# A third PSUM bank for the attention scores, taken from the projections, and a later place for one normalisation

## Chip, cores and metric

The kernel runs on one core of a Trainium2 chip. The metric is the device time of one launch in microseconds (us), the median of several runs. A core has five engines that run side by side, each with its own queue of instructions: TensorE (PE in the profile; its weight loads are listed apart as PEld), VectorE (DVE), ScalarE (ACT), GpSimd (POOL) and SyncE (SP), which issues most DMAs. TensorE writes its results to PSUM, which has eight banks; each bank here holds one tile of 128 partitions by 512 float32.

## What is computed

One hybrid decoder layer on 2048 tokens of width 1024. The normalised input is projected once; one part of the columns goes to a stick-breaking attention with 16 heads of 64, the other to a chunked state-space mixer (SSD). Each branch is gated and normalised, and one output projection adds both to the input. Cut to what matters here:

```python
hn = rmsnorm(x, norm_w)
q, k, v, z_sb, z_ssd, xBC, dt_raw = split(hn @ w_in)
q = rmsnorm(q per head, q_norm_w); k = rmsnorm(k per head, k_norm_w)
z = einsum(q, k) * 0.125                      # per head, strictly causal
log_keep = where(mask, log_sigmoid(-z), 0)
rest = reverse_cumsum(log_keep) - log_keep
w = where(mask, exp(log_sigmoid(z) + rest), 0)
o_sb = einsum(w, v)
y_sb = rmsnorm(o_sb * silu(z_sb), sb_norm_w)
y_ssd = rmsnorm((ssd(xBC, dt_raw) + D * xs) * silu(z_ssd), ssd_norm_w)
out = x + concat(y_sb, y_ssd) @ w_out
```

## The kernel before

Tokens are handled in two halves H of 1024 tokens. The order of the stages is: preparation of the first half's input; SSD of the first half (convolutions, chunks, then the gate projections of that branch, L778 to L782); attention for both halves (L449 to L713); SSD of the second half; output projection in two branches (`out_part`, L727), the attention's first.

**PSUM.** All tiles of PSUM come from four rings of banks, L30: `z` has two banks, `t` two, `av` one, `pj` three. A tile takes the next bank of its ring, and its first matmul waits until the last reader of the tile that had the bank before is done. In attention, `z` holds scores, `t` transposes, `av` the output of a head, `pj` projections. Outside, `z` and `pj` also serve the convolutions (pairs of tiles, by turns in `pj` and `z`, L294), `z` both products of an SSD chunk (`yd` and `yo`, L395 and L396), `pj` all tiles of the output's first branch and, by turns with `z`, those of the second (L757, L801, L805).

**Attention** runs over 32 segments (H, p, q): half H, pair p of heads (8 pairs), and q, the first or second 512 tokens of the half. A segment handles both heads e of the pair for its 512 queries, against all blocks c of 512 keys up to its own, so a segment has 8, 16, 24 or 32 steps, for Q = 2H+q from 0 to 3. A step i consists of

- `z_step` (L594): the scores in a `z` bank by two matmuls (L601, L602; on the diagonal a third, L604); two sigmoids by ScalarE, `be` to SBUF (L606) and one in place in the bank (L607); a scan by VectorE that reads the bank and writes the weights `w` (L610). The scan is the last reader of the `z` bank.
- `t_step` (L615), six steps later (LAG): four transposes of `w` into a `t` bank (L619), read by a rounding copy on ScalarE, `th` (L622), and by a subtraction on VectorE, `tl` (L624), the last reader of the bank.
- `av_step` (L632), two more steps later: two matmuls into `av` (L636, L637). At a head's end ScalarE and VectorE read it out (L642, L643), and POOL multiplies by the gate `gz` (L644).

**The fill.** Between steps, small pieces of work for the next two segments are issued by a generator, `fill_for` (L563), at a pace that the planner at L664 to L705 sets from costs and due times written by hand; at a segment's end the rest is drained (L706). For the segment after next it runs `stage_a` (L456): four projection tiles in `pj`, 24 matmuls each (L473 to L475); each tile is read by three operations of ScalarE (L478 to L480), and VectorE sums squares (L481). At its end come DMAs of shifted values `vd` and a subtraction on POOL (L498), then the reciprocal roots (`rsqrt`, L98, on VectorE: L103, L104, and three rounds of L106 to L108, on 128x16) and the scaling of q and k by them (L502, 128x1024, in place). For the next segment it runs `gate` (L505), 24 matmuls to one `pj` tile, whose readers are L511 and L512; `gz` has two buffers. `stage_b` (L515) transposes and weighs q and k (L524 to L531). In the second half's segments with q=0 and p under 6, `gates1` adds two `pj` tiles for the SSD gate.

In a segment whose next one has q=1, the fill begins with the gate; then come 12 steps of `stage_a`, `stage_b`, and the rest. In the others it begins with the 12 steps of `stage_a`. POOL subtracts the rounded from the full weights as they arrive (L133).

The framework sets the order of instructions on each engine when the program is built. Program order gives the priority; an instruction whose operands or bank are not free by the framework's reckoning lets later ones of the same engine go first. On the chip each engine then keeps that order.

Of the kernel before, what the change touches and what calls it, by code (L numbers as in the profile page):

```python
# [26 lines left out]

V_QW, V_KW, V_CW, V_CB, V_D, V_SBW, V_SSW, V_AL, V_DTB, V_NW, V_N = 0, 1, 2, 50, 62, 70, 78, 86, 102, 118, 126

PSB = {"z": 2, "t": 2, "av": 1, "pj": 3}  # L30
LAG = 6
NA = 12
WKB = 6
# [13 lines left out]
def hybrid_layer_kernel(ctx: ExitStack, tc: tile.TileContext, x, norm_w, wA, wP0, wP, wZ, wdt, vec, w_out, out):  # L47
# [50 lines left out]
    def rsqrt(pool, ss, n, inv, tag):  # L98

        xv = pool.tile([P, n], F32, name=tag + "x")  # L100
        y = pool.tile([P, n], F32, name=tag + "y")
        t = pool.tile([P, n], F32, name=tag + "t")
        ve.tensor_scalar(xv, ss, inv, EPS, ALU.mult, ALU.add)  # L103
        ve.tensor_scalar(y.bitcast(I32), xv.bitcast(I32), -0.5, 1597463007.0, ALU.mult, ALU.add)  # L104
        for _ in range(3):
            ve.scalar_tensor_tensor(t, xv, -0.5, y, ALU.mult, ALU.mult)  # L106
            ve.tensor_mul(t, t, y)
            ve.scalar_tensor_tensor(y, t, 1.5, y, ALU.add, ALU.mult)  # L108
        return y
# [340 lines left out]
    def attention(ap_, wp, hp, hx):  # L450

        segs = [(H, p, q) for H in range(2) for p in range(NP) for q in range(2)]
        made, wts, wzs, rows, vrs, gzs = {}, {}, {}, {}, {}, {}
        hx1, nw1 = [], []

        def stage_a(H, p, q):  # L456
# [7 lines left out]
            raw = ap_.tile([P, 4, 256], F32, name="raw", bufs=2)  # L464
            ss = ap_.tile([P, 4, 4], F32, name="ss", bufs=2)

            n = 400 if (H, p) == (1, 0) else 384
            for t in range(4):
                pj = ps("pj")
# [15 lines left out]
            vd = ap_.tile([P, 4, P], F32, name="vd", bufs=1)  # L485
# [11 lines left out]
                nc.sync.dma_start(vb_d[p:p + 1, :], vr[P - 1:P, 3, :])  # L497
            gp.tensor_sub(vd, vr, vd)  # L498
            vrs[H, p] = vr
            r = rsqrt(ap_, ss.rearrange("p t g -> p (t g)"), 16, 1.0 / 64, "qk")  # L500
            rv = raw.rearrange("p t (g d) -> p (t g) d", d=64)
            ve.tensor_tensor(rv, rv, r.unsqueeze(2).broadcast_to([P, 16, 64]), op=ALU.mult)  # L502
            rows[H, p, q] = (vd, raw)

        def gate(H, p, q):  # L505
            if q == 0:
                wzs[H, p] = load_z(wp, p, 512, "z", 2, True)
            pj = ps("pj")
            yield from projector(hx if H == 0 else hx1)[1](pj, wzs[H, p], slice(0, P), q)
            gz = ap_.tile([P, 512], F32, name="gz", bufs=2)  # L510
            sc.activation(gz, pj, AF.Sigmoid)  # L511
            ve.tensor_mul(gz, pj, gz)  # L512
            gzs[H, p, q] = gz

        def stage_b(H, p, q):  # L515

            vd, raw = rows.pop((H, p, q))

            AB = [ap_.tile([P, 2, 512], F32R, name="AB", bufs=4) for _ in range(2)]
            M = [ap_.tile([P, 512], F32R, name="M", bufs=4) for _ in range(2)]  # L520
# [42 lines left out]
        def fill_for(n):  # L563
            H, p, q = segs[n]
            if n + 1 == len(segs):
                return
            nx = segs[n + 1]
            if nx[2] == 1:
                yield from gate(*nx)
            rest = iter(())  # L570
            if n + 2 < len(segs):
                nn = segs[n + 2]
                if nn[:2] == (1, 0):
                    if nn[2] == 0:
                        nw1.extend(load_nw1(ap_))
                    xs = [scaled_x(ap_, nn[2] * 4 + i, nw1) for i in range(2)]
                    yield from stage_b(*nx)
                    yield from prep1(nn[2], hp, ap_, nw1, xs, hx1)
                rest = stage_a(*nn)
                for _ in range(NA if n else 0):  # L580
                    next(rest)
                    yield
            if nx not in made:
                yield from stage_b(*nx)
            if nx[2] == 0:
                yield from gate(*nx)
            if H == 1 and q == 0 and p < NJ:
                yield from gates1(p)
            yield from rest
# [195 lines left out]
    with tc.tile_pool(name="sp1", bufs=1, side="right") as sp:  # L785
        chunks, gates, _ = ssd(1, sp, wp, *projector(hx))
# [67 lines left out]
```

## Time and profile before

| | us |
|---|---|
| median of three runs | 2747.02 (2743.16 to 2747.48) |
| profiled execution, its own time | 2747.84 |
| its span, first to last instruction | 2745.6 |
| TensorE busy | 2592.6 (94%) |
| VectorE busy | 2016.6 (73%) |
| ScalarE busy | 1647.5 (60%) |
| GpSimd busy | 845.8 (31%) |

The granted TensorE clock is 0.988 of full speed as a mean over the span. Attention takes from about 345 to 2108 us, the first half of it up to about 1000. Times of instructions are counted from the span's start. A matmul's listed duration overlaps the next one's: two matmuls with 512 columns start 0.23 us apart, while each is listed with some 0.4 us. So a stage in which TensorE is shown as busy all the time can still have room, and the weight loads (PEld) with the idle time before them show better where it waits.

### The profile page before, as it was taken

The numbers are of one execution on the slowest core, as the hardware profiler recorded it, in microseconds if no ns is written. First come the engines' busy times: TensorE is split into PE (matmuls) and PEld (weight loads), VectorE is DVE, ScalarE is ACT, GpSimd is POOL, SyncE is SP. The second block draws the span as 40 slices with busy tenths as digits, with TensorE's granted clock in tenths as the row PEclk, the third lists the DMA queues.
The fourth block names the chain that finished last, engine by engine and source line by source line (L and its number), as shares of the span: only waits on it lengthen the run. The fifth ranks groups of instructions, "written<-read, shape, count | busy, mean of one in ns | idle before, by whom it ended". The sixth has DMA issues, their size and how long they took to land.

```text
span 2745.6 us, 40149 instructions
## 1 busy us (share of the span) xinstructions
PE 2592.6 (94%) x13858; PEld 2138.9 (78%) x13858; DVE 2016.6 (73%) x3160; ACT 1647.5 (60%) x3551; POOL 845.8 (31%) x844
## 2 busy tenths in 40 slices
PE   7998999999999999999999999999999896989999
PEld 5876788888888778787878787877776774778877
DVE  6566337767776777968696868688997667877766
ACT  4557446666666666868686867677886456331221
POOL 1456232322333222121212121212112456351553
PEclk9999999999999999999999999999999998999999
DMA  3225642222322422122212121222121136574553
GB/s 114 62 74 144 228 122 65 78 76 83 93 81 86 116 73 70 58 81 58 81 55 85 53 86 51 84 56 74 57 70 39 49 94 184 184 219 146 153 166 115
DMA packets 207627, 265.16 MB, mean 97 GB/s; under 512 B 18384, under 2 KB 127200, under 8 KB 207424
## 3 DMA queue, kind: packets, MB, share of 16 engines
q1 hardware_dynamic: 188992, 229.04, 28.1%
q10 hardware_dynamic: 18432, 33.56, 4.2%
q8 instruction: 109, 1.79, 0.3%
q14 instruction: 94, 0.77, 0.1%
HBM read 178.00 MB, written 59.38 MB: 86 GB/s over the span
## 4 chain that ended last, share of the span: by engine, by line
PE 53%; DVE 25%; issue 7%; ACT 7%; DMA 4%; POOL 3%; SPq 0%; ACTq 0%; DVEq 0%; POOLq 0%
DVE w L610 8%; PE t L619 5%; PE pj L475 4%; PE pj L474 4%; PE pj L473 4%; DVE tl L624 4%; PE pj L247 3%; PE pj L246 3%; PE pj L245 3%; PE av L636 3%; PE z L601 3%; PE av L637 2%; PE z L602 2%; PE pj L762 2%; PE pj L760 2%
## 5 line engine op out<-in xcount | busy, mean ns | idle before, releaser
L610 DVE TENSOR_TENSOR_SCAN w<-z,w,be 128x512 f32<-128x512 f32 x384 | 490.7, 1278 | 135.1 <-ACT z L607 132.5
L606 ACT ACTIVATE be<-z 128x512 f32<-128x512 f32 (+3 forms) x640 | 343.7, 537 | 328.9 <-PE z L604 166.0
L624 DVE TENSOR_TENSOR tl<-t,th 128x512 fp32r<-128x512 f32 (+3 forms) x640 | 376.9, 589 | 9.5 <-ACT th L622 7.6
L622 ACT CAST th<-t 128x512 fp32r<-128x512 f32 (+3 forms) x640 | 339.0, 530 | 31.8 <-PE t L619 29.5
L619 PE MATMUL t<-ident,w 128*128 128x128 f32 x2176 | 346.6, 275 | 9.8 <-DVE tl L624 3.8
L473 PE MATMUL pj<-wh,hh 128*128 128x384 f32 (+1 forms) x1024 | 349.9, 342 | 0.0
L475 PE MATMUL pj<-wh,hl 128*128 128x384 f32 (+1 forms) x1024 | 346.8, 339 | 0.0
L474 PE MATMUL pj<-wl,hh 128*128 128x384 f32 (+1 forms) x1024 | 346.7, 339 | 0.0
L607 ACT ACTIVATE z<-z 128x512 f32<-128x512 f32 (+3 forms) x640 | 341.1, 533 | 0.2
L610 DVE TENSOR_TENSOR_SCAN w<-z,be 128x128 f32<-128x128 f32 (+3 forms) x256 | 209.8, 819 | 170.3 <-ACT z L607 141.3
L619 PEld LDWEIGHTS t<-ident,w 128*128 128x128 f32 x2176 | 255.1, 141 | 71.7 <-DVE tl L624 16.7
L133 POOL TENSOR_TENSOR wl<-wraw,wh 128x384 fp32r<-128x384 f32 (+3 forms) x163 | 169.4, 1050 | 440.8 <-ACT wh L132 238.7
L644 POOL TENSOR_TENSOR y<-y,gz 64x512 f32<-64x512 f32 x64 | 82.9, 1296 | 531.1 <-DVE y L643 530.6
L473 PEld LDWEIGHTS pj<-wh,hh 128*128 128x128 f32 x1024 | 192.9, 188 | 12.5 <-ACT hh L173 0.2
L474 PEld LDWEIGHTS pj<-wl,hh 128*128 128x128 f32 x1024 | 193.0, 189 | 12.0
L475 PEld LDWEIGHTS pj<-wh,hl 128*128 128x128 f32 x1024 | 193.0, 188 | 0.7
L246 PE MATMUL pj<-hl,zh 128*128 128x512 f32 x432 | 175.3, 406 | 0.0
L245 PE MATMUL pj<-hh,zh 128*128 128x512 f32 x432 | 173.3, 401 | 0.0
L247 PE MATMUL pj<-hh,zl 128*128 128x512 f32 x432 | 172.2, 399 | 0.0
L636 PE MATMUL av<-th,V 128*128 128x512 f32 (+2 forms) x384 | 155.3, 405 | 12.1 <-DVE y L643 11.2
L601 PE MATMUL z<-M,AB 128*128 128x512 f32 (+2 forms) x384 | 141.4, 368 | 10.7 <-DVE w L610 8.5
L637 PE MATMUL av<-tl,V 128*128 128x512 f32 (+2 forms) x384 | 141.1, 368 | 0.0
(244 smaller groups left out, 6060.5 us busy)
## 6 DMA issues: line engine op xcount, KB each, us to landing
wraw<-in_wP_dram SPq DMA_DIRECT2D x112, 192.0 KB, 2.5
wk<-acs_scr SPq DMA_DIRECT2D x64, 256.0 KB, 3.4
AB<-AB SPq DMA_DIRECT2D x128, 128.0 KB, 2.4
Mc<-kc_scr ACTq DMA_DIRECT2D x64, 256.0 KB, 2.7
Vc<-vc_scr ACTq DMA_DIRECT2D x64, 256.0 KB, 2.6
wraw<-in_wZ_dram SPq DMA_DIRECT2D x54, 256.0 KB, 2.6
wraw<-in_wA_dram SPq DMA_DIRECT2D x44, 192.0 KB, 2.3
ea<-acs_scr SPq DMA_DIRECT2D x32, 256.0 KB, 4.4
```

What stands on the lines that cost most here:

```text
L245: te.matmul(pj[:m], a, hh[q][:, kt, :], start=(kt == 0), stop=False)
L246: te.matmul(pj[:m], a, hl[q][:, kt, :], start=False, stop=False)
L247: te.matmul(pj[:m], b, hh[q][:, kt, :], start=False, stop=(kt == KT - 1))
L473: te.matmul(pj[:, :n], a, wh[kt][:, 0:n], start=(kt == 0), stop=False)
L474: te.matmul(pj[:, :n], a, wl[kt][:, 0:n], start=False, stop=False)
L475: te.matmul(pj[:, :n], b, wh[kt][:, 0:n], start=False, stop=(kt == KT - 1))
L606: sc.activation(be[:, :nk], zp[:, :nk], AF.Sigmoid, scale=0.125)
L607: sc.activation(zp[:, :nk], zp[:, :nk], AF.Sigmoid, scale=-0.125)
L610: ve.tensor_tensor_scan(w[:, 0:nk][:, ::-1], zp[:, 0:nk][:, ::-1], be[:, 0:nk][:, ::-1], 0.0 if diag else prev[i][:, 0:1], ALU.mult, ALU.add)
L619: te.transpose(tp[:, i * P:(i + 1) * P], ws[i][:, j * P:(j + 1) * P], ident)
L622: sc.copy(th[:, rs], tp[:, rs])
L624: ve.tensor_tensor(tl[:, rs], tp[:, rs], f32(th[:, rs]), op=ALU.subtract)
```

## The change

The ring `z` gets three banks and `pj` two. The roots and the scaling at the end of `stage_a` become a function of their own, `norm_rows`. For q=0 it is called where it stood. For q=1 it is called at the beginning of the fill of the next segment (the one before the segment that the rows belong to), ahead of that segment's gate.

```diff
-PSB = {"z": 2, "t": 2, "av": 1, "pj": 3}
+PSB = {"z": 3, "t": 2, "av": 1, "pj": 2}
...
             gp.tensor_sub(vd, vr, vd)
             vrs[H, p] = vr
+            rows[H, p, q] = (vd, raw, ss)
+
+            if q == 0:
+                norm_rows(H, p, q)
+
+        def norm_rows(H, p, q):
+            vd, raw, ss = rows[H, p, q]
             r = rsqrt(ap_, ss.rearrange("p t g -> p (t g)"), 16, 1.0 / 64, "qk")
             rv = raw.rearrange("p t (g d) -> p (t g) d", d=64)
             ve.tensor_tensor(rv, rv, r.unsqueeze(2).broadcast_to([P, 16, 64]), op=ALU.mult)
-            rows[H, p, q] = (vd, raw)
...
-            vd, raw = rows.pop((H, p, q))
+            vd, raw, _ = rows.pop((H, p, q))
...
             nx = segs[n + 1]
             if nx[2] == 1:
+                norm_rows(*nx)
                 yield from gate(*nx)
```

## Rows read from the trace of the kernel before

**Rows 1.** The page's part 1: busy time, share, instructions of each engine.
```profile
PE 2592.6 (94%) x13858; PEld 2138.9 (78%) x13858; DVE 2016.6 (73%) x3160; ACT 1647.5 (60%) x3551; POOL 845.8 (31%) x844
```

**Rows 2.** Windows by stage: length, then busy us of PE, PEld, DVE, ACT, POOL.
```profile
345.00:920.00 575.00, 559.46 (x3263) 502.18 (x3262) 397.02 (x675) 357.12 (x863) 177.09 (x208) 1.00 0.30 85
1000.00:1890.00 890.00, 857.90 (x4769) 716.33 (x4767) 704.98 (x1012) 653.82 (x1406) 180.91 (x203) 1.00 0.24 69
1890.00:2108.00 218.00, 208.72 (x1124) 160.13 (x1123) 193.96 (x264) 171.57 (x358) 23.85 (x33) 1.00 0.19 53
```

**Rows 3.** PEld's waits: 1000 to 1880, 1880 to 2108, whole span (us, times, longest).
```profile
PEld z L601 <- DVE w L610: 59.8, 110, 1.9
...
PEld z L601 <- DVE w L610: 26.1, 55, 1.0
...
PEld t L619 <- DVE tl L624: 16.7, 46, 1.4
```

**Rows 4.** Windows in one head pair, a segment's end and the next head; columns as rows 2.
```profile
1428.00:1448.00 20.00, 18.49 (x95) 13.41 (x94) 19.90 (x35) 16.89 (x37) 9.29 (x11) 1.00 0.23 68
1448.00:1466.00 18.00, 18.00 (x104) 15.89 (x103) 10.91 (x15) 12.42 (x27) 4.68 (x5) 1.00 0.37 109
```

**Rows 5.** Timeline, DVE then PEld, at a segment's end: start, us, engine, instruction, [idle before].
```profile
1375.81 1.27 DVE L610 TENSOR_TENSOR_SCAN w<-z,w,be 128x512 f32<-128x512 f32 x1
1377.00 0.67 DVE L624 TENSOR_TENSOR tl<-t,th 128x512 fp32r<-128x512 f32 x1
1377.58 1.27 DVE L610 TENSOR_TENSOR_SCAN w<-z,w,be 128x512 f32<-128x512 f32 x1
...
1377.13 0.19 PEld L601 LDWEIGHTS z<-M,AB 128*128 128x128 f32 x1 [0.43 <-DVE w L610]
...
1377.71 0.48 PEld L619 LDWEIGHTS t<-ident,w 128*128 128x128 f32 x4
```

**Rows 6.** Timeline of DVE: the chain of roots for q=1, and the scan after it.
```profile
1431.64 0.17 DVE L103 TENSOR_SCALAR qkx<-ss 128x16 f32<-128x16 f32 x1
...
1440.72 1.20 DVE L502 TENSOR_TENSOR raw<-raw,qky 128x1024 f32<-128x1024 f32 x1
...
1442.44 1.27 DVE L610 TENSOR_TENSOR_SCAN w<-z,w,be 128x512 f32<-128x512 f32 x1
```

**Rows 7.** Timeline of DVE and POOL: L106 beside a weight subtraction and alone.
```profile
467.20 1.02 DVE L106 SCALAR_TENSOR_TENSOR qkt<-qkx,qky 128x16 f32<-128x16 f32 x1
...
469.42 0.17 DVE L106 SCALAR_TENSOR_TENSOR qkt<-qkx,qky 128x16 f32<-128x16 f32 x1
...
1449.08 1.02 POOL L133 TENSOR_TENSOR wl<-wraw,wh 128x384 fp32r<-128x384 f32 x1 [0.98 <-ACT wh L132]
```

**Rows 8.** PE's waits over the whole span: the SSD chunks' score bank.
```profile
PE z L412 <- DVE ea L419: 19.6, 10, 7.1
```

**Rows 9.** Timeline of PE and DVE in the output's first branch.
```profile
2438.49 0.47 PE L760 MATMUL pj<-hh,yh 128*128 128x512 f32 x1
...
2448.79 0.75 DVE L763 SCALAR_TENSOR_TENSOR res<-pj,roy,res 128x512 f32<-128x512 f32 x1
...
2449.59 0.80 PE L760 MATMUL pj<-hh,yh 128*128 128x512 f32 x1 [5.32 <-DVE res L763]
```

**Rows 10.** Timeline of PE and ACT in a first-half segment with q=0.
```profile
484.46 0.42 PE L473 MATMUL pj<-wh,hh 128*128 128x384 f32 x1
...
485.28 0.27 ACT L480 COPY vr<-pj 128x128 f32<-128x128 f32 x1
...
494.12 0.60 ACT L511 ACTIVATE gz<-pj 128x512 f32<-128x512 f32 x1 [1.87 <-POOL y L644]
```

**Rows 11.** Timeline of PE and DVE in a second-half segment with q=0.
```profile
1326.69 0.39 PE L245 MATMUL pj<-hh,zh 128*128 128x512 f32 x1
...
1330.36 0.69 DVE L512 TENSOR_TENSOR gz<-pj,gz 128x512 f32<-128x512 f32 x1 [0.62 <-ACT gz L511]
```

**Rows 12.** Timeline of ACT: a gate copy of the first half's SSD.
```profile
322.40 0.59 ACT L435 COPY zr<-pj 128x512 f32<-128x512 f32 x1 [8.30 <-DMA gss_scr<-zr]
```

## The prediction

> **What bounds the kernel now.** I read the page first: TensorE is busy 94% of the span, VectorE 73%, ScalarE 60%, GpSimd 31% [rows 1]. As matmuls overlap, the windows by stage say more [rows 2]. In attention's first half (345 to 920 us) TensorE loads weights 502 of 575 us and VectorE works 397: TensorE is the bound. In the second half (1000 to 1890) VectorE works 705 of 890 us, in the last two pairs (1890 to 2108) 194 of 218: there the bound changes inside each segment. Next, the waits: weight loads of the score matmuls (z) wait for the scan that frees a z bank, 59.8 us in 110 places between 1000 and 1880 and 26.1 us in 55 places after that, 86 us in all; over the whole span the transposes (t) wait only 16.7 us for `tl` [rows 3]. Windows inside one head pair (1328 to 1467 us) show the two regimes [rows 4]: at the end of a segment, when its fill has run out, VectorE works 19.90 of 20 us; at the head of the next, with dense fill, 10.91 of 18.
>
> **What a z wait is worth.** In the timeline of such an end [rows 5] one scan ends at 1377.08, z is loaded at 1377.13 after 0.43 us of idling; but the next transposes, at 1377.71, follow the end of a `tl` at 1377.67. That `tl` frees their t bank (two of them, L30). The step is 1.77 us (scan to scan), all VectorE's. With a third z bank z goes earlier, the transposes can't, and the period stays. I made this comparison for all 165 z waits after 1000 us; in 121 of them the transposes start within 0.15 us of the release of their bank. Where they start later, the smaller of wait and slack adds up to 11 us. So the third bank is worth between 0 and 11 us by this reading, 86 us if no other wait took over. I take 6.
>
> **The moved roots.** The chain L103 to L108 (11 small operations) and the scaling L502 is emitted for q=1 at the next segment's start instead of after its projections. It issues no DMA and moves past none; SP's and POOL's orders don't change by it; `vd` and its DMAs stay. What is behind it on VectorE are scans and `tl`. In [rows 6] it lies in the saturated end: from 1431.64 to the scan at 1442.44 are 10.80 us, in which five scans pass. At 1.77 us each, less 0.4 for one short `tl`, these need 8.5. So 2.3 us come free per such chain. It stands so in six segments (starts 1154 to 1848, one per pair; a seventh, 1977, moves within a stretch that is full everywhere, and those of the first half lie where VectorE has room). That is 6 x 2.3 = 14 us, at most 7 x 2.96 (its own time) = 21, at least 0 if the chain lands again among saturated scans. What it costs at the new place: the head leaves VectorE 18 - 10.9 = 7.1 us idle [rows 4]. But POOL subtracts weights there, from 1449.08 on, and beside such a subtraction an L106 took 1.02 us, alone 0.17 [rows 7]; chains in the first half, beside POOL, own 5.5 to 6.9 us. 5.5 still fit into 7.1. I cost it at nothing; what hides it is the wait of scans for the dense fill, and if that cover is gone it costs what it owns, 3 to 5.5 us a pair. The scaled q, k are wanted only 20 fill steps later.
>
> **Score banks outside attention.** The SSD chunks take yd and yo from z too; there z waits 19.6 us for `ea` [rows 8]. Three banks let the next group's yd start early, but these chunks also wait for ScalarE's exponentials and DMAs. Between 0 and 19.6 I take 5. The convolutions alternate z and pj in pairs, so one gains what the other loses: nothing.
>
> **The bank taken from the projections.** With three pj banks there is one TensorE wait, 5.3 us [rows 9]. The question is when three tiles were alive. I took each tile's first matmul and its last reader:
> - First half, segments with q=0: the gate tile's sigmoid waits for POOL's y and runs at 494.12, long after its matmuls [rows 10]. Until then four projection tiles share what is left: three banks leave two, two leave one. The tile at 484.46 starts while its predecessor is read until 485.55: 1.09 us. Such overlaps are 2.23, 1.09, 1.07 in each of six pairs, 26 us in all.
> - Second half: gates1's first tile starts at 1326.69, the gate tile before it is released at 1331.05, so 4.36 us [rows 11]; with 1.6 and 0.9 beside it 6.9 us, six times: 41 us.
> - These waits cost only if TensorE has nothing else. Instructions are ordered by readiness: at the end shown in [rows 4] the timeline has matmuls of the next segment's gate between score matmuls. Attention steps, 1.3 us of matmul work each, can go between two tiles. In the second half a fill pushed towards the saturated end costs nothing. Of 67 us I take 4.
> - First output branch: all tiles are pj. The tile at 2438.49 starts 11 us before the one at 2427 is released, 2449.54 [rows 9]; part of that is today's 5.3 us. The net loss here is 5.6 us, with a second such place (2468) near 10; the overlaps there sum to 28. I take 6.
> - First half's SSD gates: copies wait up to 8.30 us for the earlier store [rows 12]; overlaps sum to 14 us in five places. I take 4, since chunks fill some.
>
> **Sum**, against the profiled execution (2747.8 us, span 2745.6): -14 -6 -5 +4 +6 +4 = -11, so 2737. It stands 0.8 above the median, hence 2736.
>
> **Rivals.**
> 1. *Two banks serialise the projections* (slower). With the gate tile holding one bank, each projection waits for the predecessor's three ScalarE reads. For: [rows 10 to 12], and TensorE has no slack in the first half. Against: work that can go between. In full: 26 + 41 + 11 + 14 = 92 us; at half, with the gains of 25, +21: 2769. It decides from about a third of the 92 on. The Trainium skill, "Perfetto Trace Analysis", Matmuls, asks that independent matmul groups rotate through PSUM banks so that the evacuation of one overlaps the next group's matmuls; by that rule, taken strictly, the 92 us are lost: 92 - 25 = +67, 2814. No stretch of the trace shows pj at work with one bank, so it stays open. Chance 0.25.
> 2. *The chain isn't moved.* The ordering may pull these VectorE operations back among the saturated scans, as it does with the gate's matmuls. Then the 14 us don't come and the sum is +3: 2750. Chance 0.2.
> 3. *The z waits vanish.* If the transposes' 0.04 us in [rows 5] is only order and not a limit, most of the 86 us go: with half to three quarters of them the time is 2665 to 2710. The Trainium skill, "Perfetto Trace Analysis", Optimization Strategy, says that the same gap repeating on the engine that should be saturated can mean too few PSUM buffers; by that rule z's repeated gap would go with the third bank. Against it stands that in 121 of the 165 cases the t bank had just come free. Chance 0.1.
>
> **How the numbers follow.** My forecast, 2722 to 2743, has 0.45. A measurement tells some 0.2%, 5.5 us, from no change. Faster than 2741.5: nearly all of the forecast, rival 3, little of rival 2, 0.51. Within 0.2%: most of rival 2 and the rest of the forecast, 0.23. Slower: rival 1 and the tail of rival 2, 0.26. These have both signs, so the range reaches from the gains' far bounds (14 for the chain, 11 for the bank, 10 for chunks, no loss: -35, 2712) to rival 1 at somewhat under half (2766). The likeliest case's own range is 2722 to 2743.
>
> **What would show it.** Right: L502 of q=1 stands at the head of the next segment, beside idle scans; z waits on scans fall well under 86 us, and waits of t on `tl` rise by most of that; a pair of the second half is 2 to 3 us shorter than its 139. Wrong: TensorE waits at L473 or L245 for ScalarE's readers of pj, first-half pairs longer than now (rival 1); L106 to L108 of q=1 still between saturated scans (rival 2); t waits that stay near 17 us while pairs shrink by 5 or more (rival 3); output tiles that wait for L763 for over 15 us.

## The result, and the profile after

The change makes the kernel slower: 2775.32 us (median, 2773.84 to 2776.93) against 2747.25 for the kernel before, a ratio of 1.0107, 95% interval 1.0094 to 1.012. The forecast was 2736, its range 2712 to 2766: the sign was wrong, and the time lies 9 us above the range.

The new version's lines lie six or seven further down from L502 on: the scan is L617 (before L610), the subtraction for `tl` L631 (L624), the scores L608 (L601), the scaling of q and k L509 (L502), the output's sum L770 (L763). First the busy times, from the page's part 1, to be set beside [rows 1]:

```profile
PE 2617.0 (94%) x13858; PEld 2140.1 (77%) x13858; DVE 2025.3 (73%) x3160; ACT 1640.1 (59%) x3551; POOL 841.8 (30%) x844
```

The instructions are the same in number, and no engine has more than 1% more work, VectorE and the weight loads under 0.5%. What has grown, by 26.5 us (span 2772.1 against 2745.6), is time in which TensorE waits or goes on at a lower density (its listed busy time holds 24.4 us more for the same matmuls). The next table says where. It is worked out from the timelines of both kernels: the first stage ends where the first projection matmul L473 starts, a segment with the last addition to `y` (L643 before), and the means are over pairs 1 to 5 of the first half and 1 to 4 of the second, counted from 0, which differ among themselves by at most 0.4 us. In the stretches of these pairs the granted clock is 1.00 in both kernels. The addition that marks a segment's end comes some 21 us behind the first score matmul of the next segment, so work can move across the mark, and what counts in the second half is the sum of the two segments of a pair.

| us | before | after | difference |
|---|---|---|---|
| to the start of attention | 346.6 | 350.4 | +3.8 |
| attention | 1756.7 | 1780.1 | +23.4 |
| – of it, one pair of the first half | 76.70 | 78.23 | +1.53 |
| – of it, a first segment (q=0) of the second half | 63.53 | 65.04 | +1.51 |
| – of it, a second segment (q=1) there | 75.34 | 75.58 | +0.24 |
| from the end of attention | 642.3 | 641.6 | -0.7 |

**The projections wait.** In the first half, weight loads for L473 now wait for ScalarE's reading of an older projection tile, three times in a pair. These are the three places in the timeline of the weight loads (PEld) in one pair of the changed kernel; the bracket is the idle time before the load and what ended it. In between are lines without such a wait:

```profile
562.14 0.19 PEld L473 LDWEIGHTS pj<-wh,hh 128*128 128x128 f32 x1 [0.81 <-ACT vr L480]
...
568.46 0.19 PEld L473 LDWEIGHTS pj<-wh,hh 128*128 128x128 f32 x1 [0.41 <-ACT vr L480]
...
575.17 0.19 PEld L473 LDWEIGHTS pj<-wh,hh 128*128 128x128 f32 x1 [0.22 <-ACT vr L480]
```

They add up to 1.44 us, against the 1.53 by which the pair is longer. So there the loss is in plain sight.

**The scores' waits have become the transposes'.** PEld's waits in the changed kernel, first from 1020 to 1914 us, then to 2136 (about the same work as in the first two of [rows 3]; total us, times, longest), and at last three rows of the whole span:

```profile
PEld z L608 <- DVE w L617: 51.7, 78, 1.7
PEld t L626 <- DVE tl L631: 27.4, 58, 1.1
...
PEld z L608 <- DVE w L617: 17.2, 37, 1.0
PEld t L626 <- DVE tl L631: 9.7, 25, 0.9
...
PEld z L608 <- DVE w L617: 75.3, 121, 2.5
PEld t L626 <- DVE tl L631: 44.3, 98, 1.1
...
PEld pj L473 <- ACT vr L480: 12.1, 25, 1.1
```

Waits of z fell from 86 us to 51.7 + 17.2 = 69. Waits of t on `tl` grew over the whole span from 16.7 to 44.3. The 17 us gained at z are more than taken back at t.

**The chain of roots has stayed at the segment's end.** The timeline of VectorE in the changed kernel, with the first operation of a second segment's chain, one of the scans between, the last operation, and the scaling:

```profile
1452.71 0.18 DVE L103 TENSOR_SCALAR qkx<-ss 128x16 f32<-128x16 f32 x1
...
1457.66 1.27 DVE L617 TENSOR_TENSOR_SCAN w<-z,w,be 128x512 f32<-128x512 f32 x1
...
1469.05 0.15 DVE L108 SCALAR_TENSOR_TENSOR qky<-qkt,qky 128x16 f32<-128x16 f32 x1
1469.24 1.23 DVE L509 TENSOR_TENSOR raw<-raw,qky 128x1024 f32<-128x1024 f32 x1
```

Nine scans pass between L103 and L509, eight of the old segment and the first of the new one, where five passed in [rows 6]: the chain is spread more thinly, but still among the scans of the end. Windows of the changed kernel around such an end (the new segment's first score matmul starts at 1464.48) and for the head after it (length, then busy us of PE, PEld, DVE, ACT, POOL, as in [rows 4]) show the two regimes as before:

```profile
1451.00:1471.00 20.00, 18.27 (x95) 13.09 (x96) 19.86 (x34) 15.86 (x36) 7.07 (x9) 1.00 0.12 31
1471.00:1491.00 20.00, 19.56 (x109) 16.61 (x108) 13.60 (x18) 14.25 (x30) 7.68 (x9) 1.00 0.42 128
```

VectorE is full in the end (19.86 of 20 us) and has room in the head, which is where the chain was meant to run.

### The profile page after: what moved, and what is told of

Its sections match the earlier page's. It is cut to its first block, busy times and chain, and to the rows that moved or that the text cites. A ratio compares the mean times of both kernels' runs of the same rounds, so it can differ in the third digit from the quotient of the medians.

```text
span 2772.1 us, 40308 instructions
## 1 busy us (share of the span) xinstructions
PE 2617.0 (94%) x13858; PEld 2140.1 (77%) x13858; DVE 2025.3 (73%) x3160; ACT 1640.1 (59%) x3551; POOL 841.8 (30%) x844
## 4 chain that ended last, share of the span: by engine, by line
PE 55%; DVE 23%; ACT 7%; issue 6%; DMA 5%; POOL 3%; SPq 0%; ACTq 0%; DVEq 0%; POOLq 0%
DVE w L617 6%; PE t L626 5%; PE pj L473 5%; PE pj L475 5%; PE pj L474 5%; PE pj L245 4%; PE pj L246 4%; PE pj L247 4%; DVE tl L631 3%; PE av L643 3%; PE av L644 2%; PE z L608 2%; PE z L609 2%; PE pj L767 2%; PE pj L769 2%
## 5 line engine op out<-in xcount | busy, mean ns | idle before, releaser
L617 DVE TENSOR_TENSOR_SCAN w<-z,w,be 128x512 f32<-128x512 f32 x384 | 490.4, 1279 | 132.4 <-ACT z L614 129.4
L631 DVE TENSOR_TENSOR tl<-t,th 128x512 fp32r<-128x512 f32 (+3 forms) x640 | 376.8, 590 | 14.9 <-ACT th L629 12.5
L473 PE MATMUL pj<-wh,hh 128*128 128x384 f32 (+1 forms) x1024 | 352.8, 344 | 5.9 <-ACT vr L480 4.2
L475 PE MATMUL pj<-wh,hl 128*128 128x384 f32 (+1 forms) x1024 | 347.4, 339 | 0.0
L617 DVE TENSOR_TENSOR_SCAN w<-z,be 128x128 f32<-128x128 f32 (+3 forms) x256 | 209.0, 819 | 171.8 <-ACT z L614 144.9
L626 PEld LDWEIGHTS t<-ident,w 128*128 128x128 f32 x2176 | 251.4, 141 | 89.1 <-DVE tl L631 44.3
L133 POOL TENSOR_TENSOR wl<-wraw,wh 128x384 fp32r<-128x384 f32 (+3 forms) x163 | 169.5, 1052 | 458.1 <-ACT wh L132 254.0
L473 PEld LDWEIGHTS pj<-wh,hh 128*128 128x128 f32 x1024 | 193.1, 189 | 24.5 <-ACT vr L480 12.1
L475 PEld LDWEIGHTS pj<-wh,hl 128*128 128x128 f32 x1024 | 192.8, 188 | 1.5
L245 PE MATMUL pj<-hh,zh 128*128 128x512 f32 x432 | 174.4, 404 | 0.0
L247 PE MATMUL pj<-hh,zl 128*128 128x512 f32 x432 | 172.1, 398 | 0.0
L643 PE MATMUL av<-th,V 128*128 128x512 f32 (+2 forms) x384 | 156.3, 407 | 14.8 <-DVE y L650 14.1
L608 PE MATMUL z<-M,AB 128*128 128x512 f32 (+2 forms) x384 | 141.3, 368 | 6.6 <-DVE w L617 4.1
```

Source lines behind the costliest of these rows:

```text
L245: te.matmul(pj[:m], a, hh[q][:, kt, :], start=(kt == 0), stop=False)
L247: te.matmul(pj[:m], b, hh[q][:, kt, :], start=False, stop=(kt == KT - 1))
L473: te.matmul(pj[:, :n], a, wh[kt][:, 0:n], start=(kt == 0), stop=False)
L475: te.matmul(pj[:, :n], b, wh[kt][:, 0:n], start=False, stop=(kt == KT - 1))
L617: ve.tensor_tensor_scan(w[:, 0:nk][:, ::-1], zp[:, 0:nk][:, ::-1], be[:, 0:nk][:, ::-1], 0.0 if diag else prev[i][:, 0:1], ALU.mult, ALU.add)
L626: te.transpose(tp[:, i * P:(i + 1) * P], ws[i][:, j * P:(j + 1) * P], ident)
```

## The experiments

Twelve kernels, each timed against the kernel before. `attn` is the length of attention, first the time to its start and last the time behind it, all three from the traces by the same marks as above; the stage to the start of attention differs by 2 us (344.5 to 346.6) among six kernels in which nothing of it was changed, so differences of that size mean nothing there. Behind attention the spread among the same six is 4.8 us (637.5 to 642.3), and the three pairs of the first half that are not in the means add up to anything between 318.6 and 323.9. So a difference of up to 5 us in the whole of attention means little where the pairs don't show it too. The kernel before was timed again beside each group of runs, with medians of 2745.49 us (e1 to e4), 2744.07 (e5 to e8) and 2747.27 (e9 to e12); between groups, ratios compare, and not times.

| run | ratio [95%] | to attn | attn | behind | first-half pair | second half q=0 / q=1 |
|---|---|---|---|---|---|---|
| before | 1 | 346.6 | 1756.7 | 642.3 | 76.70 | 63.53 / 75.34 |
| after (the change) | 1.0107 [1.0094, 1.012] | 350.4 | 1780.1 | 641.6 | 78.23 | 65.04 / 75.58 |
| e1 banks only | 1.0079 [1.0066, 1.0092] | 349.9 | 1772.1 | 642.4 | 78.18 | 65.02 / 74.64 |
| e2 roots only | 1.0000 [0.9989, 1.001] | 344.9 | 1761.6 | 641.6 | 76.71 | 63.53 / 75.26 |
| e3 roots tied | 0.9977 [0.9967, 0.9988] | 344.9 | 1751.8 | 638.4 | 76.73 | 63.51 / 74.25 |
| e4 two pj banks only | 1.0111 [1.0094, 1.0128] | 350.9 | 1774.6 | 645.5 | 78.41 | 65.14 / 74.61 |
| e5 gate in z | 1.0066 [1.0054, 1.0078] | 350.3 | 1767.8 | 647.7 | 76.69 | 64.05 / 76.28 |
| e6 spread over z | 1.0163 [1.0146, 1.018] | 378.2 | 1764.4 | 644.0 | 76.70 | 63.82 / 76.08 |
| e7 roots tied, new banks | 1.007 [1.0057, 1.0083] | 347.4 | 1765.8 | 641.8 | 78.28 | 65.00 / 73.76 |
| e8 roots tied, old banks, 1.25 | 0.9952 [0.9941, 0.9964] | 346.4 | 1745.3 | 639.0 | 76.70 | 62.39 / 74.48 |
| e9 before with 1.25 | 1.0028 [1.0018, 1.0039] | 344.7 | 1769.4 | 639.1 | 76.73 | 62.39 / 77.82 |
| e10 roots tied, old banks, 1.15 | 0.9938 [0.9924, 0.9951] | 344.5 | 1741.5 | 637.5 | 76.67 | 63.54 / 72.93 |
| e11 gate's own bank | 1.0039 [1.0026, 1.0051] | 350.6 | 1757.7 | 647.2 | 76.73 | 63.86 / 75.33 |
| e12 third bank to t | 1.0061 [1.0048, 1.0073] | 352.6 | 1765.2 | 644.7 | 78.07 | 63.78 / 74.98 |

### The change in its parts: e1, e2 and e4

**e1** is the kernel before with the new banks alone:

```diff
-PSB = {"z": 2, "t": 2, "av": 1, "pj": 3}
+PSB = {"z": 3, "t": 2, "av": 1, "pj": 2}
```

> The kernel before with z 3 and pj 2 banks, the roots left where they were. Theory A (the bank costs, the moved roots do nothing because the ordering puts them back): as slow as the changed kernel, 2775 us, within 5. Rival B (the moved roots cost, by scans that wait behind them): near 2750 to 2760, the rest comes with the roots. In the first half's pairs theory A expects 1.4 us more a pair, all of it TensorE's wait for the last ScalarE reader of pj (L480).

**e2** has the moved roots alone, with the old banks (the rest of the diff ahead of the prediction).

> The kernel before with the roots of q=1 called in the next segment's fill, banks as before (z 2, pj 3). Theory A: no change, 2747 us, within 4, because the chain L103 to L108 still stands between the scans of the segment's saturated end. Rival B: 2765 or more. The prediction's term for the moved roots alone would give 2733.

**e4** takes the bank from the projections and gives it to nobody:

```diff
-PSB = {"z": 2, "t": 2, "av": 1, "pj": 3}
+PSB = {"z": 2, "t": 2, "av": 1, "pj": 2}
```

> The kernel before with pj 2 and z 2, one bank of PSUM unused. Theory A (the taken pj bank is the whole cost and the third z bank gives next to nothing, as the transposes' banks come free at the same time): 2775 us, within 5, and the same as with z 3. Rival C (the third z bank gives some 10 to 20 us and the pj bank costs 40 or more): 2785 to 2800. Rival D (z 3 itself costs, by another order of fill and scores): 2755 to 2765.

Measured: e1 2766.13 us, e2 2745.87, e4 2775.49. e1 and e4 divide attention's 23.4 us into steps: taking the bank from the projections costs 1774.6 - 1756.7 = 17.9 us (e4), giving it to the scores returns 1774.6 - 1772.1 = 2.5 (e1), and moving the roots on top of that costs 1780.1 - 1772.1 = 8.0 (the changed kernel against e1). Taken one after the other like this, steps always add up to the whole, so the sum tests nothing; e2 shows that moving the roots does less harm with the old banks. So the third bank for the scores is worth next to nothing in attention, 0.1 us in a pair of the second half and 0.2 in one of the first, and the projections' third bank is worth far more than that. Over the whole kernel the scores' bank brings more: the ratios of e4 and e1, 1.0111 and 1.0079, lie 9 us apart, and of the 6.6 us between their profiled executions 4.1 fall outside attention. Of the expectations, e2's theory A held, and e1 came out between its two; e4's theory A had the time right, but not that it would be the same as with the scores' third bank. PEld's waits of e1 from 1000 us to attention's end show the same exchange as the changed kernel's:

```profile
PEld z L601 <- DVE w L610: 64.0, 122, 1.3
PEld t L619 <- DVE tl L624: 32.0, 64, 1.4
```

and those of e4 in the same stretch:

```profile
PEld z L601 <- DVE w L610: 95.3, 178, 1.6
...
PEld t L619 <- DVE tl L624: 9.0, 35, 0.7
```

The sums, 96.0 and 104.3 us, differ by 8 us where the z waits alone differ by 31.

In e2 the chain lies where it does in the changed kernel, among the scans. Start and end of it in VectorE's timeline:

```profile
1434.08 0.17 DVE L103 TENSOR_SCALAR qkx<-ss 128x16 f32<-128x16 f32 x1
...
1449.55 0.14 DVE L108 SCALAR_TENSOR_TENSOR qky<-qkt,qky 128x16 f32<-128x16 f32 x1
1449.73 1.23 DVE L509 TENSOR_TENSOR raw<-raw,qky 128x1024 f32<-128x1024 f32 x1
```

From 1434.08 to 1450.87 lie nine scans. The later place in the program is a lower priority; that this is why the small operations end up thinly among the scans is a reading of the order, and not shown by a run. Pairs of the second half are 0.08 us shorter, which is nothing.

### The roots where the change's text puts them: e3 and e7

**e3** has the moved roots with the old banks, and ties the chain of a second segment behind the latest scan that has been issued, which is the first scan of the new segment (diff against e2).

```diff
-            r = rsqrt(ap_, ss.rearrange("p t g -> p (t g)"), 16, 1.0 / 64, "qk")
+            with tc.issue_after(scans[-1]) if q == 1 and scans else ExitStack():
+                r = rsqrt(ap_, ss.rearrange("p t g -> p (t g)"), 16, 1.0 / 64, "qk")
...
-            ve.tensor_tensor_scan(w[:, 0:nk][:, ::-1], zp[:, 0:nk][:, ::-1], be[:, 0:nk][:, ::-1],
+            sc_ = ve.tensor_tensor_scan(w[:, 0:nk][:, ::-1], zp[:, 0:nk][:, ::-1], be[:, 0:nk][:, ::-1],
...
+            scans.append(sc_.ins)
```

> As the one before, but VectorE's chain of roots is tied behind the first scan issued in the new segment, so that it can't be put among the earlier segment's last scans. If the term for the moved roots was right and only the ordering undid it, 6 chains x 2.3 us come free: 2733 us, and segments with q=1 of the second half are 2 us shorter than 75.3. If a full VectorE at a segment's end is not what sets its length, or the head pays it back: 2747, within 4.

Measured: 2740.2 us, 0.23% faster than before, with the interval below 1; that is between the two times expected. VectorE's timeline of e3 has the chain at the head, the scan of the new segment's diagonal block ahead of it:

```profile
1441.88 0.41 DVE L618 TENSOR_TENSOR_SCAN w<-z,be 128x128 f32<-128x128 f32 x1
1442.20 0.14 DVE L103 TENSOR_SCALAR qkx<-ss 128x16 f32<-128x16 f32 x1
...
1447.76 1.22 DVE L510 TENSOR_TENSOR raw<-raw,qky 128x1024 f32<-128x1024 f32 x1
```

So the move is worth something, but 4.9 us in attention and not 14. Why so little can be read from windows of the same length as the end of such a segment, from its last projection matmul (L473 to L475) to the next segment's first score matmul: 17.2 us in the kernel before (1428.3 to 1445.5), 15.3 in e3 (1424.4 to 1439.7). First the row of before, then, in a fence of its own, that of e3:

```profile
1428.30:1445.50 17.20, 15.97 (x81) 11.45 (x79) 17.10 (x32) 14.53 (x31) 7.11 (x9) 1.00 0.21 65
```

```profile
1424.40:1439.70 15.30, 14.41 (x76) 10.15 (x73) 14.94 (x20) 13.99 (x31) 6.01 (x8) 1.00 0.18 57
```

The end is 1.9 us shorter, near the 2.3 that the prediction works out. But in the kernel before TensorE does 12 matmuls of the next segment's gate (L245 to L247) in these 17.2 us, in e3 5. The seven that are left over are done in the head, where TensorE is the bound; at 0.23 us each, the distance of two matmuls with 512 columns, that would be 1.6 us. Of the 1.9 us the pair keeps 63.53 + 75.34 - 63.51 - 74.25 = 1.1. Where the other 0.8 us go shows when the stretch around the border is divided, for the kernels with and without the moved roots (us, medians of the second segments of pairs 1 to 4; the end is from the end of the last projection matmul to the next segment's first score matmul, the head from there to the segment's mark):

| run | end | gate matmuls in it | head |
|---|---|---|---|
| before | 16.42 | 12 | 21.48 |
| e2, roots moved | 15.27 | 5 | 22.40 |
| e3, moved and tied | 14.49 | 5 | 22.34 |
| e1, new banks | 14.65 | 10 | 22.29 |
| after, roots moved | 14.29 | 3 | 23.53 |
| e7, moved and tied | 12.62 | 3 | 23.38 |

In all four kernels with moved roots seven gate matmuls have left the end, and the head is 0.9 to 1.2 us longer than without. It is not the small operations of the chain that make it longer: all eleven lie in the head in e3 and e7, but only three in e2 and four in the changed kernel, each of 0.14 to 0.17 us (in the pairs whose chains are shown). What all four have there is the seven matmuls and the scaling, 1.2 us of VectorE. As VectorE has room in the head, the matmuls are the likelier cause, but no run separates the two.

**e7** has the same tie in the changed kernel, with its new banks.

> The changed kernel with its new banks, and the chain of the roots tied behind the first scan of the new segment, so that it stands where the change's code puts it. Theory (the 9 us between the run with the banks alone and the changed kernel come from the chain's ordering among the scans of the segment's end, and not from the idea of moving it): 2766 minus about 5, as the tie gave 5 without the banks, so about 2760, and a pair of the second half about 1 us shorter than in the changed kernel. Rival (the 9 us come from running the chain later at all, because fewer gate matmuls then fill the segment's end): the pair stays as in the changed kernel and the time within 3 us of 2775.

Measured: 2762.13 us, a ratio of 1.007, clear of the changed kernel's 1.0107; from e1's 1.0079 the intervals don't tell it apart. The second segments are 1.8 us shorter than in the changed kernel and 0.9 shorter than in e1. The last table says how. Against e1 the head grows by about the same in both, 1.2 us in the changed kernel and 1.1 in e7, while the end gets 2.0 us shorter in e7 and only 0.4 in the changed kernel. So the move costs the head something wherever the chain lands, and with the new banks it pays only if the chain leaves the end. The net loss in the changed kernel's attention thus belongs to the place that the ordering chose for the chain, and not to the idea of running it later; the rival of the expectation falls.

### Who needs the third projection bank: e5, e6 and e11

**e5** is e1 with the gate's tile of second segments in the scores' ring.

```diff
-            pj = ps("pj")
+            pj = ps("z" if q else "pj")
```

> Banks changed (three for the scores, two for the projections), roots where they were before, and the gate's projection of a pair's second segment takes a bank of the scores' ring in place of a projection bank. Theory (the projections lose their time because the gate's tile holds one of the two projection banks for the whole of its filling, so that the projections of the next pair have a single bank left): a pair of the first half goes back from 78.2 us towards the 76.7 of the kernel before, a first segment of a pair of the second half from 65.0 towards 63.5, and the time is some 10 to 15 us under the 2766 of the run with the banks alone, about 2753. Rival (two banks are too few for the q, k, v projections themselves, whoever else uses them): a pair of the first half stays at 78.2 and the time at 2766, or above it where the gate's tile now takes a bank from the scores.

Measured: 2762.08 us. The pair of the first half is back at 76.69, as the theory has it, to 0.01 us. First segments of the second half gain 1.0 of the 1.5. But second segments lose 1.6 against e1, so that the pair is 0.7 longer, and the whole gains some 4 us, not 10 to 15; the intervals of e5 and e1 overlap. PEld's waits of e5, from 1000 us to attention's end, show the gate's tile itself waiting for scans:

```profile
PEld z L601 <- DVE w L610: 65.8, 115, 1.5
PEld t L619 <- DVE tl L624: 37.3, 82, 1.5
...
PEld z L245 <- DVE w L610: 4.3, 9, 0.5
```

In the second half a bank lent by the scores is not free: the 4.3 us at L245 and 5.3 more at t than in e1 are the rival's part.

**e11** separates the two. One of the three projection banks is taken out of the ring and kept for the gates of second segments; all else is the kernel before.

```diff
-PSB = {"z": 2, "t": 2, "av": 1, "pj": 3}
+PSB = {"z": 2, "t": 2, "av": 1, "pj": 2, "gb": 1}
...
-            pj = ps("pj")
+            pj = ps("gb" if q else "pj")
```

> The kernel before with one of its three projection banks taken out of the ring and kept for the gates of second segments alone; two banks for the scores, roots where they were. Theory (the loss of the projections with two banks is the gate's tile, which holds one of them for its whole filling): 76.7 us for a pair of the first half and 63.5 and 75.3 for the two segments of a pair of the second half, as in the kernel before; only the first stage and the last keep their loss, so about 2752 to 2755. Rival (q, k and v need the third bank themselves): 78.2 and 65.0 as with two banks, 2770.

Measured: 2757.25 us, with 76.73, 63.86 and 75.33 in attention, which is 1.0 us longer in all than in the kernel before, where e4 is 17.9 longer. So in the first half q, k and v do with two banks; what they can't do with is one bank, and one is what the gate's tile leaves them while it is filled between other work and waits for its readers. That is [rows 10] read to its end: the gate's reader L511 came at 494.12, long after its matmuls. The remaining loss, 10 us, is outside attention, where the ring is two banks again and the gates' own bank lies unused: 4.0 in the first stage, and 4.9 behind attention, which is about the spread there. In e11's first stage one gate matmul waits 5.7 us for ScalarE's copy, [rows 12]'s line L435:

```profile
PEld pj L245 <- ACT zr L435: 5.7, 1, 5.7
```

**e6** is the changed kernel with all other users of `pj` lent a bank from `z`: the gates of second segments and of `gates1` as a whole, the first stage's gates and the first output branch by turns.

```diff
-            pj = ps("pj")
+            pj = ps(("pj", "z")[q] if m == P else "pj")
...
-        out_part(op0, op0, 0, ("pj",), wo)
+        out_part(op0, op0, 0, ("pj", "z"), wo)
```

> The changed kernel whole, and the users of the projection ring other than q, k and v spread over both rings: the gates of second segments and of the last stage's chunks go to the scores' ring, the gates of the first stage and the sums of the first output half take the two rings in turn. Theory (all of the loss of the smaller ring is waits for a bank, 25 us over the stages by the run with one bank unused): the first stage ends at about 345 to 347 us in place of 350, a pair of the first half takes 76.7 in place of 78.2, the last stage comes back by 3, and the time is 2750 to 2757, of which 5 to 9 over the kernel before are left for the moved roots. Rival (the scores' waits grow by as much when their ring is lent): 2770 or more.

Measured: 2787.86 us, the slowest of all. Attention is 15.7 us shorter than in the changed kernel, near what the theory wanted, but the first stage is 27.8 longer. There the SSD chunks take both their products from `z`, and a gate tile now stands between them. PEld's waits in the first stage of e6, 60 to 380 us:

```profile
PEld z L416 <- DVE ea L419: 28.2, 11, 6.6
```

In e1, with the same rings and the gates in `pj`, it is (60 to 352 us):

```profile
PEld z L416 <- DVE ea L419: 9.1, 10, 2.9
```

The waits are 19 us longer, against 27.8 us of the stage. For the rest there is one sign. From 260 to 300 us the granted clock was 0.81 in e6, so some two fifths of that stretch were at the lower of the two levels, 1.2 GHz, after 40 us in which TensorE was busy for 28.43; in the changed kernel it was 1.00, after 40 us with 35.86. What that took is not shown. A ring shared with slow readers hands their delay on to the others, whichever ring it is. The expectation was a miss on this stage.

### Where the bank could have gone: e12

```diff
-PSB = {"z": 2, "t": 2, "av": 1, "pj": 3}
+PSB = {"z": 2, "t": 3, "av": 1, "pj": 2}
```

> Two banks for the scores, two for the projections, and the bank that is left given to the ring of the transposes (three in place of two); roots where they were. Theory (the waits for a bank in the second half are VectorE's, which frees the scores' banks by its scans and the transposes' banks by its copies, so a bank more only changes which of the two TensorE waits for): second-half pairs within 0.5 us of the run with the eighth bank unused (65.1 and 74.6 us), waits of the transposes shorter and those of the scores longer, the whole 2765 to 2775. Rival (with three scores' banks the transposes' ring was what then held TensorE, so it is the one that wanted the bank): pairs at least 2 us shorter, 2755 or less.

Measured: 2763.28 us. Attention is 9.4 us shorter than with the bank unused (e4), where the scores' bank brought 2.5; a pair of the second half has 138.76 against 139.75, where e1 has 139.66. Over the whole kernel the intervals of e12 and e1 overlap, as e12 is slower outside attention. Neither side of the expectation holds: pairs are neither within 0.5 us nor 2 us shorter. And the prediction that z would wait longer was wrong. PEld's waits of e12 from 1000 us to attention's end, to be set beside e4's rows above:

```profile
PEld z L601 <- DVE w L610: 76.6, 153, 1.4
...
PEld t L619 <- DVE tl L624: 5.5, 9, 1.0
```

Both are shorter, 95.3 to 76.6 and 9.0 to 5.5. So VectorE isn't all that holds the second half, and of the two rings it is the transposes' that gains by a bank in attention. Which of its users does, whether the steps' or those of L524 (`stage_b`), was not tried. First segments of the second half are back at 63.78, as they are in e11 (63.86), though here the gate's tile shares two projection banks as in e4 (65.14). So in the second half a bank for the transposes makes up for that loss as well as one for the gate does; whether it takes the same loss away or brings a gain of its own is not shown. A pair of the first half stays at 78.07.

### The room in the ends: e8, e9 and e10

If a head that TensorE bounds is what the dense fill lengthens, then spreading the fill further into the end should pay once the chain has left the end, and only then. The planner's factor for the second half (`FF`) sets how fast the fill is spent. A lower factor spends it more slowly, so more of it is left for the end: the last projection matmul of a second segment ends 37.4 us behind the mark at which the segment starts in e3, 41.9 in e8 and 44.7 in e10. The expectation of e8 has this direction the wrong way round; its times don't hang on it. **e8** is e3 with a lower factor, **e9** the kernel before with the same one, **e10** e3 with one lower still.

```diff
-FF = (1.05, 1.35)
+FF = (1.05, 1.25)
```

> The run with the tied chain and the old banks (2740), with the factor of the planner for the second half lowered from 1.35 to 1.25, which spends the next segment's matmuls earlier and leaves fewer for the head. Theory (what a segment's end gives back is the number of gate matmuls that TensorE can do there: the kernel is TensorE-bound in heads, VectorE-bound in ends): more work planned into the ends, second-half pairs shorter by up to 1 us each, 2733 to 2738. Rival (the planner's factor already balances the two ends, so that earlier matmuls only delay scores): 2740 or slower, up to 2750.

> The kernel before with nothing but the planner's factor for the second half lowered from 1.35 to 1.25. Theory A (what the tied chain gives and what the factor gives are separate, each by where the fill is done): the factor alone gives the 8 us that lay between the run with the tied chain and the run with both, so about 2737. Theory B (the factor pays only where the chain has left the segment's end, since in the kernel before that end is full on VectorE): 2744 or slower, and second-half pairs of 138.5 us or more.

> The tied chain and the old banks once more, with the planner's factor for the second half at 1.15 in place of 1.25 and 1.35. If what limits the pair is TensorE in the head, with room left in the segment's end: another 4 to 8 us less, 2724 to 2728. If the room in the ends is used up at 1.25: 2732 or slower, with first segments of a pair shorter and second segments longer by as much or more.

Measured: e8 2731.95 us, e9 2754.03, e10 2729.92. The same edit takes 6.5 us off attention with the tied chain (e8 against e3) and adds 12.7 without it (by the ratios of the whole kernel, 7 and 8), so theory B of e9 holds: pairs there have 62.39 + 77.82 = 140.2 us. In e8 first segments are 1.1 us shorter than in e3 and second segments only 0.2 longer. What the slower fill costs a second segment differs, because in e9 the chain is still in the end. Windows of 20 us at the end of the same segment (columns as above) show how much TensorE does there. In e9 TensorE is busy 16.50 us, and the second segments are 2.5 us longer than before:

```profile
1430.00:1450.00 20.00, 16.50 (x86) 12.41 (x85) 18.71 (x31) 16.08 (x34) 9.66 (x11) 1.00 0.28 79
```

In e10 it is busy 19.66 us, with 111 matmuls in place of 86 and as much work of VectorE beside it:

```profile
1416.00:1436.00 20.00, 19.66 (x111) 16.38 (x111) 18.71 (x24) 18.80 (x43) 9.28 (x11) 1.00 0.27 80
```

e10's time lies between the two that were expected, and the intervals (0.9924 to 0.9951 and 0.9941 to 0.9964) don't tell it from e8. Its segments moved against the second expectation, first segments 1.1 us longer than in e8 and second segments 1.5 shorter. Either beats both kernels; e10 is 0.6% below the kernel before, and 1.7% below the changed one. It has the change's second part, tied in place, and a slower fill, without the first part.

## Why the prediction was wrong

By the ratios over the whole kernel, the bank taken from the projections cost 30 us (e4) where the prediction has 4 + 4 + 6 = 14; the bank given to the scores returned 9 (e1 against e4) where it has 11; the moved roots brought nothing with the old banks (e2) and cost 8 with the new ones (the changed kernel against e1) where it has a gain of 14.

**The bank taken from the projections** is the step that failed most: "Attention steps, 1.3 us of matmul work each, can go between two tiles. [...] Of 67 us I take 4." Attention lost 17.9 (e4). The place was named; but the discount to 4 rested on no row. In the first half 1.7 us of 4.4 overlapping in a pair were lost, since TensorE is the bound there and its order is set when the program is built: a load at L473 that waits for L480 holds all that stands behind it. In the second half first segments lost 1.6 and second segments won 0.7 back, so a pair lost 0.9. Only 3.0 us of the changed kernel's waits at L473 fall into the second half, so most of the loss there isn't seen as a wait for a bank. A bank of the gate's own takes most of it away (e11 has 0.3 of the 0.9 left), and a third bank for the transposes makes up for it (e12); by which path is open. The Trainium skill, "Perfetto Trace Analysis", Matmuls, wants independent matmul groups to rotate through PSUM banks. The trace agrees in kind, with 12.1 us of waits at L473 where there were none; in size it is 17.9 us of attention and not the whole overlap of 67.

**The moved roots**, "6 x 2.3 = 14 us", came out as nothing alone (e2) and as a loss of 8.0 in attention with the new banks. Two things failed. The ordering kept the chain among the scans, which was rival 2. And where it is tied in place the end does get 1.9 us shorter, near the 2.3, but what the new place costs, which was put at nothing, is 0.9 us in e3's head. It is not the reason that was weighed, the chain beside POOL's subtractions, since e2's head is as long with only three of the eleven small operations in it; it goes with the seven gate matmuls that left the end. Idle time of one engine in a stage bound by another is used by something; the term should have been charged for it.

**The third score bank in attention**, -6 between 0 and -11: measured -2.5 (e1 against e4), which is within the spread of attention, and 0.1 to 0.2 us by pairs. The mechanism was right: z waits fell well under 86, t waits on `tl` rose by more, and the pairs hardly changed. The Trainium skill, "Perfetto Trace Analysis", Optimization Strategy, takes a repeating gap on the engine that should be saturated as a possible lack of buffers. Here the gap was TensorE's, 86 us of it, and a bank for the ring that showed it took away 17 at the gap and 2.5 of the time; a bank for the ring that hardly showed one, t, was worth 9.4 in attention (e12). That last is what the reading of [rows 5] pointed to and the prediction didn't follow up.

**The first stage**, +4: measured +3.8, and +4.3 with two score banks. **Chunks and output branch**, -5 and +6, together +1: measured -0.7. By e4 and e1, +3.2 for the projections' bank and -3.1 for the scores'. These are no larger than the spread behind attention, so only the signs have support: that stretch is 644.7 to 647.2 us in the three runs with two projection and two score banks (e4, e11, e12), and at most 642.3 in the six with the old ones. The granted clock moves there too, from a mean of 0.97 before to 0.96 after, and no run separates that from the banks. The waits of [rows 8], 19.6 us at L412, are now 12.7 us at L416; those for the output's sum [rows 9] rose from 5.3 to 10.3. PE's waits over the whole span, after:

```profile
PE z L416 <- DVE ea L419: 12.7, 9, 4.3
...
PE pj L767 <- DVE res L770: 10.3, 3, 6.3
```

**The rivals and the range.** Rivals 1 and 2 both came true. Each was priced with the other's gain still standing: rival 1 at half kept the chain's 14 us, and rival 2 kept the projections at +4. Rival 1 at half without the 14 is 2783, and the changed kernel lies below that, outside a range that ended at "somewhat under half" with the 14 kept. One is about banks, the other about order, and neither excludes the other, so a joint case was due a chance of its own. The full price of rival 1 also takes 11 us for the first output branch, where the overlaps are said to sum to 28, and doesn't say why. The signs named were the right ones to look for: waits at L473 for ScalarE, first-half pairs longer, L106 to L108 still between scans.

## What to carry to other kernels

Before a bank is taken from a ring, look for its longest-lived tile, not its busiest: a tile that is filled in pieces and waits for its readers takes a bank out of the rotation, and three banks with one such tile are two. When work is moved in the program, see in the trace whether the order of the engine moved with it, and charge the gain with what other engines did in the time that goes away. A wait that repeats names the ring that is waited for, and here the shorter one was another; if one engine frees both, try the other ring too.

## What was not expected of the hardware

POOL is slowed by VectorE as VectorE is by POOL. In e3's timeline of POOL three subtractions L133 take 2.95 us, 0.98 each, and the next one 1.92:

```profile
1443.90 2.95 POOL L133 TENSOR_TENSOR wl<-wraw,wh 128x384 fp32r<-128x384 f32 x3 [3.54 <-ACT wh L132]
1447.94 1.92 POOL L133 TENSOR_TENSOR wl<-wraw,wh 128x384 fp32r<-128x384 f32 x1 [1.08 <-ACT wh L132]
```

It starts at 1447.94, inside the scaling L510 (1447.76 to 1448.98, shown above with e3); from the end of that to its own end at 1449.86 are 0.88 us, less than its usual length. Beside the three before it a VectorE operation on 128x16 took 0.93 us; the next of that size, started when POOL was idle, took 0.17:

```profile
1445.95 0.93 DVE L107 TENSOR_TENSOR qkt<-qkt,qky 128x16 f32<-128x16 f32 x1
1446.92 0.17 DVE L108 SCALAR_TENSOR_TENSOR qky<-qkt,qky 128x16 f32<-128x16 f32 x1
```

The Trainium skill, "SBUF — State Buffer", Who interferes with whom, says that a VectorE instruction with two SBUF inputs contends with a GpSimd instruction that reads SBUF, that their shared ports are an exclusive lock, and that the order of issue decides who blocks. The rows agree, with 1.92 us for 0.98 and 0.93 for 0.17: each engine's operation lasts about as long as the other's rest and its own together.
